# Gated attention: head 1's first half moved ahead of head 0's second half, with the norm of the second half of x between its products

## The chip, the cores and the metric

The kernel runs on one core of a Trainium2 chip. The metric is the time of one execution in device microseconds (us). Before the change the median of three runs is 2456.72 us (2456.72 to 2458.53).

## What is computed

The reference is a trunk of two layers on x (1024 tokens by 1024 features, float32). Layer 0 uses gated linear attention, layer 1 differential softmax attention; each is followed by a squared-ReLU MLP, and every sub-layer is normed and modulated by a conditioning vector. The change lies in layer 0's attention, with four heads, 128 key columns (DK) and 256 value columns (DV) each:

```python
h = rmsnorm(x, norm_g[i, 0]) * (1.0 + scale_t) + shift_t
q, k, v, r, a_lr = jnp.split(h @ w_in, [hk, 2 * hk, 2 * hk + D_MODEL, 2 * hk + 2 * D_MODEL], axis=-1)
log_a = jax.nn.log_sigmoid((a_lr @ w_a2 + b_a).astype(f32)) / GLA_TAU
...
b = jnp.cumsum(chunks(log_a, dk), axis=2)
scores = jnp.where(causal, jnp.einsum('bnchk,bnshk->bnhcs', q_dec, k_intra), 0.0)
o_intra = jnp.einsum('bnhcs,bnshv->bnchv', scores, v)
...
    o_c = jnp.einsum('bchk,bhkv->bchv', q_c, state)
    state = state * jnp.exp(decay)[..., None] + jnp.einsum('bchk,bchv->bhkv', k_c, v_c)
...
o = rmsnorm(o, norm_g).reshape(B, T, D_MODEL) * jax.nn.silu((r + b_r).astype(f32))
```

`a_lr` (16 columns, "rank") is shared by all heads; the state runs along the tokens, so a head's second half needs the state that its first half leaves.

## The kernel before, in words

**Units.** The 1024 tokens are two halves of 512 (four tiles of 128). A unit is one head on one half: 32 value parts (`v_part`, four tiles by eight row blocks of h), eight q parts and eight k parts (`qk_part`). Every product is three matmuls (`mm3`, L117 to L120) of the two-part split of its operands. The operands are split by `split` (L113 to L115): ScalarE writes the high part (L114), VectorE the low part (L115). A unit ends with the take-overs `take_v`, `take_q`, `take_k`, the decays (`decays`, L434: a product z, log-sigmoid, a scan and four exponentials), the turn of k (`turn_k`), the scores (`score`), four steps of output and state (`out_step`, L490, matmuls po and pu) with a norm of the output at the end (L525), and two turns of the output (`out_turn`, L529) that store it in `os_`.

**Order before.** Until about 64 us the prologue computes scale and shift and norms the first half of x. Then `first_unit` (L567) does head 0's first half, with all sums open at once: four value sums, q and k. It turns the rank columns, makes the decays, and calls `second_half` (L595), which norms the second half of x: squares by ScalarE, a broadcast of the reciprocal root, and for each of eight row blocks four transposes (L604), a copy to `xc` (L606), a store of `xc` to `xs` (L607) and three operations that write `h_hi` and `h_lo` (L611 to L613). Only then do `take_q`, `take_k`, `turn_k` and `score` of the first unit follow in the program. After that `stream` (L632) yields the units (0,1), (1,0), (1,1), (2,0) to (3,1) as (head, half), and two products of the gate r.

**What sets the order.** In the stream TensorE's order is written out by hand (`manual_schedule`, L647). The `Agenda` (L51) is a planner with a clock of its own: each part adds its cost to `now`, and steps such as `turn_k` or `out_step` are put in with a lag (`GLA_LAG`, L44) and emitted when they are due. The orders of the other engines, and TensorE's outside that block, are chosen by the compiler. Each engine works in the order so fixed.

**Buffers.** Split weights have five buffers (`wsp`, L89), raw ones two (`wraw`, L90). A unit pair needs four: two value tiles, q and k; the value tiles of head 0 carry the 16 rank columns as well (`gla_v`, L242). In PSUM `mm` has two buffers, `po` two, `pu` and `sc` one each, `tr` two. The four value sums of the first unit lie in `po`, `po`, `pu`, `sc`, its q and k in `mm`. The tiles of value, of the state S, and so on have the buffer counts of the pools `gu` and `gl`; `gl` and `ga` are opened when the pool `xb`, which holds the second half of x, is closed.

**ada blocks.** Beside the stream the rest of layer 0's modulation is computed in eight blocks (`ada_next`, L622): eight loads of 256 KB on POOL's queue, eight VectorE operations into one accumulator (L216 to L218, one buffer), then transposes and a sum (`ada_sums`, L222). The next block is begun when the last one's sums are emitted, 30.5 planner units after it began.

Of the kernel before, what the change touches and what calls it, by code (L numbers as in the profile page):

```python
# [21 lines left out]
P = 128  # L22
# [60 lines left out]
def trunk(ctx: ExitStack, tc, a, out):  # L83
# [157 lines left out]

    def gla_v(hd, i, pinned=False):  # L242
        w = a["gla_w_in"][0].rearrange("(k p) n -> p k n", p=P)[:, 4 * i:4 * i + 4, :]
        c0 = 1024 + hd * DV
        more = [w[:, :, 3072:3088]] if hd == 0 else []
        return [weight([w[:, :, c0:c0 + DV]] + more, [P, 4, DV + 16 * len(more)], pinned)]
# [16 lines left out]
    with tc.tile_pool(name="xa", bufs=4, reuse_waits="tile") as xa, \  # L263
# [57 lines left out]
        for blk in range(4):  # L321
# [16 lines left out]
            if blk == 0:  # L338
                bc = mm.tile([P, HT], F32, name="bc", tag="mm")
                broadcast(bc, rstd, 4)  # L340
                for k in range(KT):
                    tr = gp2.tile([P, HT], F32, name="tr", tag="tr", bufs=2)
                    for j in range(4):
                        pe.transpose(out=tr[:, j * P:(j + 1) * P], in_=xt[j][:, k * P:(k + 1) * P], identity=ident)
                    act.copy(out=xT[k], in_=tr)
                    dve.tensor_tensor(out=xn[k], in0=xT[k], in1=bc, op=ALU.mult)
                w_v0 += gla_v(0, 0, True)
            elif blk == 1:
                w_q0 = wcols(win, 0, DK, True)
            elif blk == 2:  # L350
                w_k0 = wcols(win, 512, DK, True)
                w_v0 += gla_v(0, 1, True)
            st = gp2.tile([P, 4], F32, name="st", tag="tr", bufs=2)
# [30 lines left out]
    with gla as g:  # L384
# [24 lines left out]
        def v_part(pv, half, w_v, j, k):  # L409
            agenda.now += 0.33  # L410
            hh, hl = h[k][half]
            wh, wl = w_v[k // 4]
            mm3(pv, hh[:, tiles[j]], hl[:, tiles[j]], wh[:, k % 4, :], wl[:, k % 4, :], k == 0, k == KT - 1)

# [4 lines left out]
        def take_v(u, pv, j):  # L419
            if u["hd"] == 0:  # L420
                if j == 0:
# [57 lines left out]
        def score(u):  # L479
# [5 lines left out]
            dve.copy_predicated(out=scz[u["half"]], mask=mk.bitcast(U32).broadcast_to([P, 4, P]), data=sc)  # L485
            agenda.add(lag["out"], out_step, u, 0)

        states = {}

        def out_step(u, j):  # L490
# [9 lines left out]
            if not (half == 1 and j == 3):  # L500
# [23 lines left out]
            for j in range(4):  # L524
                dve.tensor_scalar(out=ot[:, j, :], in0=ot[:, j, :], scalar1=rs[:, j:j + 1], scalar2=None, op0=ALU.mult)  # L525
            agenda.add(lag["turn"], out_turn, u, 0)
            agenda.add(lag["turn"] + 1.0, out_turn, u, 1)

# [9 lines left out]

        def unit(hd, half, ws):

            u = dict(hd=hd, half=half, v=[])
            w_v, w_q, w_k = ws
            if hd:
                agenda.add(lag["decay"], decays, u)
            for j in range(4):
                pv = mm.tile([P, DV + 16 if hd == 0 else DV], F32, name="pv", tag="mm")
# [4 lines left out]
            if hd == 0:  # L551
                agenda.add(lag["rank"], turn_at, u)
# [13 lines left out]

        def first_unit(between):  # L567
            u = dict(hd=0, half=0, v=[])
            pvs = [gp.tile([P, HT], F32, name="pv", tag=tag, bufs=bufs)[:, :DV + 16]
                   for tag, bufs in (("po", 2), ("po", 2), ("pu", 1), ("sc", 1))]  # L570
            pq, pk = (mm.tile([P, HT], F32, name=name, tag="mm") for name in ("pq", "pk"))
            for k in range(KT):
# [4 lines left out]
            for j in range(4):  # L577
                take_v(u, pvs[j], j)
            turn_at(u)
            decays(u)  # L580
            between()
            take_q(u, pq)
            take_k(u, pk)
            turn_k(u)
            score(u)

        with tc.tile_pool(name="xb", bufs=2, reuse_waits="tile") as xb:
            xt = []
# [4 lines left out]
            for k in range(KT):  # L593
                in_order(nc.sync.dma_start(out=xs[k, :, 0:HT], in_=xT[k]))
            def second_half():  # L595
                ssq = gt.tile([P, 4], F32, name="xssq", tag="ssq")
                rstd = gt.tile([P, 4], F32, name="xrstd", tag="rs")
                token_rms(xt, gt, ssq, rstd, xb.tile([P, D], BF16, name="junk", tag="xc"))
                bc = gp.tile([P, HT], F32, name="bc", tag="po", bufs=2)
                broadcast(bc, rstd, 4)  # L600
                for k in range(KT):
                    tr = gp2.tile([P, HT], F32, name="tr", tag="tr", bufs=2)
                    for j in range(4):
                        pe.transpose(out=tr[:, tiles[j]], in_=xt[j][:, k * P:(k + 1) * P], identity=ident)  # L604
                    xc = xb.tile([P, HT], F32, name="xc", tag="xc")
                    act.copy(out=xc, in_=tr)  # L606
                    nc.sync.dma_start(out=xs[k, :, HT:T], in_=xc)  # L607
                    hi, lo = hp.tile([P, HT], F32R, name="h_hi", tag="hhi"), hp.tile([P, HT], F32R, name="h_lo", tag="hlo")
                    h[k].append((hi, lo))
                    t = gt.tile([P, HT], F32, name="xh", tag="oT")  # L610
                    dve.scalar_tensor_tensor(out=t, in0=xc, scalar=gs[:, 0, k:k + 1], in1=bc, op0=ALU.mult, op1=ALU.mult)  # L611
                    act.activation(out=hi, in_=t, func=AF.Identity, bias=mod[:, 0, k:k + 1])
                    dve.scalar_tensor_tensor(out=lo, in0=t, scalar=mod[:, 0, k:k + 1], in1=hi.bitcast(F32),  # L613
                                             op0=ALU.add, op1=ALU.subtract)

            first_unit(second_half)

# [14 lines left out]
        def stream():  # L632

            for hd in range(GLA_H):
                ws = (gla_v(hd, 0) + gla_v(hd, 1), wcols(win, hd * DK, DK), wcols(win, 512 + hd * DK, DK)) if hd else \
                    (w_v0, w_q0, w_k0)
# [743 lines left out]
```

## Time and profile before

| | |
|---|---|
| median of three runs | 2456.72 us |
| the profiled execution, its own time | 2459.76 us |
| its span, first to last instruction | 2458.0 us |
| TensorE busy | 2381.5 us (97%) |
| VectorE busy | 1672.2 us (68%) |
| ScalarE busy | 999.1 us (41%) |
| mean granted TensorE clock | 0.988 |

Engines are written PE (TensorE), DVE (VectorE), ACT (ScalarE), POOL (GpSimd), SP (which issues DMAs). A wait is shown as the idle time of an engine before an instruction, with what released it. A clock of 1.00 is 2.4 GHz, 0.50 is 1.2 GHz.

### The profile page before, as it was taken

Reading aid. Unit: us, or ns where it says so; the run is one execution under the profiler, and the core shown is the slowest. Engines: PE = TensorE matmul, PEld = TensorE weight load, DVE = VectorE, ACT = ScalarE, POOL = GpSimd, SP = SyncE. Lnnn points to the kernel's source line nnn. Section 1 sums busy time; section 2 is a strip of 40 time slices with the busy share of each in tenths; the row PEclk is TensorE's granted clock in tenths of the full one; section 3 lists DMA queues with packets and bytes.
Section 4 is the critical chain, followed back from the end, with each engine's and each line's share of the span. In section 5 each row is a group of like instructions: output and inputs, shape, how many; then the busy total and the mean of one; then the engine's idle time right before and its main releaser. Section 6 shows DMA issues by size and latency. Waiting matters only on the chain.

```text
span 2458.0 us, 33452 instructions
## 1 busy us (share of the span) xinstructions
PE 2381.5 (97%) x12215; PEld 2051.2 (83%) x12215; DVE 1672.2 (68%) x3175; ACT 999.1 (41%) x1985; POOL 271.3 (11%) x482
## 2 busy tenths in 40 slices
PE   6899999999999999999999999999999999999998
PEld 5688878887888788888999999987788888888887
DVE  7777777666655666776787878788676656555444
ACT  5655556453332321212555555565553333222111
POOL 3011100001111201211221111120001111000000
PEclk8999999999999999999999999999999999999999
DMA  8333353524333844653211111024523334633111
GB/s 294 117 120 104 102 172 111 160 95 122 114 103 104 309 137 140 213 167 118 76 41 36 35 35 35 25 83 133 167 85 119 115 106 155 214 112 112 65 43 69
DMA packets 261925, 286.58 MB, mean 117 GB/s; under 512 B 15546, under 2 KB 200032, under 8 KB 261760
## 3 DMA queue, kind: packets, MB, share of 16 engines
q1 hardware_dynamic: 237120, 206.67, 26.8%
q0 software_dynamic: 23232, 75.53, 8.9%
q8 instruction: 96, 1.57, 0.3%
q10 hardware_dynamic: 1408, 2.24, 0.2%
q14 instruction: 69, 0.57, 0.1%
HBM read 222.52 MB, written 61.87 MB: 116 GB/s over the span
## 4 chain that ended last, share of the span: by engine, by line
PE 61%; issue 21%; DMA 7%; DVE 5%; ACT 3%; POOL 2%; POOLq 0%; DVEq 0%; SPq 0%; ACTq 0%
PE acc L118 10%; PE acc L119 10%; PE acc L120 10%; DMA ada_raw<-in_ada_w 4%; PE acc L859 3%; PE acc L860 3%; PE acc L861 3%; PE pp L118 3%; PE pp L120 3%; PE pp L119 3%; POOL hs L763 1%; DMA inner<-hs 1%; PE pr L118 1%; PE pr L120 1%; PE pr L119 1%
## 5 line engine op out<-in xcount | busy, mean ns | idle before, releaser
L114 ACT CAST whi<-raw 128x1024 fp32r<-128x1024 f32 (+3 forms) x217 | 209.1, 965 | 501.7 <-PE acc L119 276.8
L718 DVE SCALAR_TENSOR_TENSOR x<-acc,mod,x 128x512 f32<-128x512 f32 (+1 forms) x312 | 222.5, 720 | 221.2 <-PE acc L120 217.7
L118 PE MATMUL acc<-h_hi,whi 128*128 128x512 f32 x896 | 352.1, 393 | 2.4 <-DVE x L718 2.3
L119 PE MATMUL acc<-h_lo,whi 128*128 128x512 f32 x896 | 350.0, 391 | 0.0
L120 PE MATMUL acc<-h_hi,wlo 128*128 128x512 f32 x896 | 349.9, 390 | 0.0
L115 DVE TENSOR_TENSOR wlo<-raw,whi 128x1024 fp32r<-128x1024 f32 (+3 forms) x217 | 243.1, 1121 | 75.1 <-ACT whi L114 71.6
L118 PE MATMUL acc<-hd,whi 128*128 128x512 f32 (+1 forms) x576 | 212.2, 368 | 2.8 <-DVE x L718 2.8
L120 PE MATMUL acc<-hd,wlo 128*128 128x512 f32 (+1 forms) x576 | 211.2, 367 | 0.0
L119 PE MATMUL acc<-hd,whi 128*128 128x512 f32 (+1 forms) x576 | 211.2, 367 | 0.0
L118 PEld LDWEIGHTS acc<-h_hi,whi 128*128 128x128 f32 x896 | 168.7, 188 | 37.1 <-DVE x L718 3.4
L120 PEld LDWEIGHTS acc<-h_hi,wlo 128*128 128x128 f32 x896 | 168.6, 188 | 35.2
L119 PEld LDWEIGHTS acc<-h_lo,whi 128*128 128x128 f32 x896 | 168.7, 188 | 33.4
L118 PE MATMUL pp<-whi,h_hi 128*128 128x384 f32 x512 | 182.8, 357 | 0.7 <-ACT v L114 0.7
L859 PE MATMUL acc<-h_hi,whi 128*128 128x512 f32 x448 | 174.8, 390 | 0.0
L860 PE MATMUL acc<-h_lo,whi 128*128 128x512 f32 x448 | 174.7, 390 | 0.0
L861 PE MATMUL acc<-h_hi,wlo 128*128 128x512 f32 x448 | 174.0, 389 | 0.0
L120 PE MATMUL pp<-whi,h_lo 128*128 128x384 f32 x512 | 172.7, 337 | 0.0
L119 PE MATMUL pp<-wlo,h_hi 128*128 128x384 f32 x512 | 172.1, 336 | 0.0
L213 POOL DMA_DIRECT2D ada_raw<-in_ada_w x160 | 86.2, 539 | 534.0 <-DVE mod L230 318.9
L218 DVE SCALAR_TENSOR_TENSOR ada_acc<-ada_raw,cact,ada_acc 128x512 f32<-128x512 f32 x140 | 104.9, 749 | 52.4 <-DMA ada_raw<-in_ada_w 51.5
L861 PE MATMUL acc<-tq,wlo 128*128 128x512 f32 x336 | 132.0, 393 | 2.1 <-DVE wlo L115 2.1
L859 PE MATMUL acc<-tq,whi 128*128 128x512 f32 x336 | 131.7, 392 | 2.2 <-ACT part L870 2.2
(1802 smaller groups left out, 5257.9 us busy)
## 6 DMA issues: line engine op xcount, KB each, us to landing
raw<-in_mlp_w SPq DMA_DIRECT2D x128, 512.0 KB, 4.2
ada_raw<-in_ada_w POOLq DMA_DIRECT2D x160, 256.0 KB, 3.4
inner<-hs SPq DMA_DIRECT2D x128, 256.0 KB, 3.6
hs<-inner POOLq DMA_DIRECT2D x112, 256.0 KB, 3.0
x<-xs SPq DMA_DIRECT2D x64, 256.0 KB, 6.3
raw<-in_gla_w_in SPq DMA_DIRECT2D x24, 512.0 KB, 3.8
xs<-x SPq DMA_DIRECT2D x48, 256.0 KB, 3.0
raw<-in_diff_w_in SPq DMA_DIRECT2D x64, 192.0 KB, 2.9
```

The lines of the kernel that those rows point to most:

```text
L114: act.copy(out=hi, in_=src)
L115: dve.tensor_tensor(out=lo, in0=src, in1=hi.bitcast(F32), op=ALU.subtract)
L118: pe.matmul(out=o, lhsT=lh, rhs=rh, start=start, stop=False)
L119: pe.matmul(out=o, lhsT=lh, rhs=rl, start=False, stop=False)
L120: return pe.matmul(out=o, lhsT=ll, rhs=rh, start=False, stop=stop)
L213: queue.dma_start(out=w, in_=a["ada_w"][l].rearrange("(k p) n -> p k n", p=P)[:, k:k + kk, c0:c0 + n])
L218: dve.scalar_tensor_tensor(out=acc, in0=w[:, j, :], scalar=cact[:, k + j:k + j + 1], in1=acc, op0=ALU.mult, op1=ALU.add)
L718: return dve.scalar_tensor_tensor(out=t, in0=psum, scalar=mcols(l, gate)[:, kt:kt + 1], in1=t, op0=ALU.mult, op1=ALU.add)
L763: pool.dma_start(out=hs[f, :, half * HT:(half + 1) * HT], in_=r)
L859: pe.matmul(out=pt, lhsT=lh, rhs=rh, start=begin and k == 0, stop=False, skip_group_check=True)
L860: pe.matmul(out=pt, lhsT=lh, rhs=rl, start=False, stop=False, skip_group_check=True)
L861: pe.matmul(out=pt, lhsT=ll, rhs=rh, start=False, stop=k == K2 - 1, skip_group_check=True)
```

## The change

Head 1's first half is computed right behind head 0's first half, before the second half of x is there; the norm of the second half is cut into agenda steps that are emitted between the products of that unit. Then the stream does (1,1), (0,1), and (2,0) to (3,1).

```diff
-GLA_LAG = dict(rank=1.09, decay=4.71, keys=3.36, score=4.04, out=7.24, step=2.16, turn=14.56, ada=30.5)
+GLA_LAG = dict(first_keys=6.5, first_score=8.5, second_decay=12.0, x_norm=3.0, x_step=1.5, held=0.5, early_turn=7.0, second_out=15.0, rank=1.09, decay=4.71, keys=3.36, score=4.04, out=7.24, step=2.16, turn=14.56, ada=30.5)
...
+    ss = dram.tile([P, DV], F32, name="ss")
...
+            if u["hd"] == 0 and u["half"] == 1:
+                S = [gl.tile([P, DV], dt, name="S", tag=f"S{i}") for i, dt in enumerate((F32, F32R, F32R))]
+                nc.sync.dma_start(out=S[0], in_=ss)
+                split(S[1], S[2], S[0])
+                states[0] = S
+            if gl is None:
+                held.append(u)
+            else:
+                agenda.add(u["out"], out_step, u, 0)
...
-                split(Sn[1], Sn[2], Sn[0])
-                states[hd] = Sn
+                if hd == 0 and half == 0 and j == 3:
+                    nc.sync.dma_start(out=ss, in_=Sn[0])
+                else:
+                    split(Sn[1], Sn[2], Sn[0])
+                    states[hd] = Sn
...
-        def first_unit(between):
+        def first_unit():
...
+            pvs = [mm.tile([P, DV + 16], F32, name="pv", tag="mm") for _ in range(2)]
+            pvs += [gp.tile([P, HT], F32, name="pv", tag="po", bufs=2)[:, :DV + 16] for _ in range(2)]
+            pq, pk = (gp.tile([P, HT], F32, name=name, tag=tag) for name, tag in (("pq", "pu"), ("pk", "sc")))
...
-            turn_at(u)
+            agenda.add(lag["rank"], turn_at, u)
+            agenda.add(2 * lag["rank"], behind_first, u, pq, pk)
+
+        def behind_first(u, pq, pk):
             decays(u)
-            between()
             take_q(u, pq)
             take_k(u, pk)
-            turn_k(u)
-            score(u)
+            agenda.add(lag["first_keys"], turn_k, u)
+            agenda.add(lag["first_score"], score, u)
...
+                agenda.add(lag["x_norm"], spread, rstd)
+
+            def spread(rstd):
+                agenda.now += 0.9
                 bc = gp.tile([P, HT], F32, name="bc", tag="po", bufs=2)
                 broadcast(bc, rstd, 4)
                 for k in range(KT):
+                    agenda.add(k * lag["x_step"], turn_x, k, bc)
...
+            first_unit()
+            second_half()
+            w1 = (whole_v(1, True, True),)
+            for k in range(KT):
+                in_order(nc.sync.dma_start(out=xs[k, :, 0:HT], in_=xT[k]))
+            w1 += rest(1)
+            with tc.manual_schedule(engines={pe.engine}):
+                for n, _ in enumerate(unit(1, 0, w1, decay=lag["second_decay"])):
+                    while agenda.due() or n == 39 and not held:
+                        agenda.run()
+                while len(h[KT - 1]) < 2:
+                    agenda.run()
...
+            yield from unit(1, 1, w1, True)
+            yield from unit(0, 1, (whole_v(0), *rest(0)))
+            for hd in range(2, GLA_H):
+                ws = (whole_v(hd), *rest(hd))
                 for half in range(2):
-                    if hd or half:
-                        yield from unit(hd, half, ws)
+                    yield from unit(hd, half, ws)
...
             ada_next()
+            for u in held:
+                agenda.add(lag["held"], out_step, u, 0)
```

`turn_x` is the body of the old loop for one row block, unchanged. `whole_v` and `rest` are the loads of a head's two value tiles and of its q and k. The rank columns now come with head 1's value tiles, as a second load; unit (1,0) multiplies the first 256 columns alone, unit (1,1) all 272, unit (0,1) no longer has them. Head 0's state after the first half goes to DRAM (`ss`) and comes back before its second half; head 0's four weight tiles are loaded and split a second time for unit (0,1). The output turns of units (0,0) and (1,0) get a lag of 7.0 instead of 14.56. The stores of the first half of x to `xs` stand behind head 1's value loads on SP's queue.

## Rows read from the trace of the kernel before

**Rows 1.** The page's first part: busy time, share of the span, instructions.

```profile
PE 2381.5 (97%) x12215; PEld 2051.2 (83%) x12215; DVE 1672.2 (68%) x3175; ACT 999.1 (41%) x1985; POOL 271.3 (11%) x482
```

**Rows 2.** Windows: stretch, length, busy by engine, granted clock, DMA share, GB/s.

```profile
64.30:101.30 37.00, 26.52 (x165) 22.04 (x164) 29.70 (x51) 22.79 (x48) 5.87 (x11) 0.91 0.44 138
102.00:135.00 33.00, 31.08 (x194) 26.56 (x194) 27.07 (x49) 21.24 (x46) 2.26 (x5) 0.98 0.38 113
320.00:346.00 26.00, 21.86 (x109) 18.23 (x108) 16.61 (x37) 13.56 (x32) 2.77 (x5) 0.87 0.65 214
```

**Rows 3.** Windows: the two stretches at the lower clock.

```profile
75.80:82.50 6.70, 5.09 (x24) 4.60 (x23) 6.70 (x12) 6.54 (x13) 1.68 (x3) 0.50 0.44 155
339.40:345.40 6.00, 5.79 (x18) 4.78 (x19) 4.94 (x10) 2.00 (x3) 1.15 (x2) 0.50 0.81 281
```

**Rows 4.** Waits of TensorE between 60 and 345 us, the two longest.

```profile
PE tro L534 <- DVE ot L525: 4.1, 1, 4.1
PE tr L604 <- ACT xc L606: 4.1, 4, 2.8
```

**Rows 5.** Timeline of TensorE: start, busy, instruction, in the attention stage.

```profile
66.29 1.12 PE L439 MATMUL z<-aT,wa 16*128 16x512 f32 x2 [1.42 <-ACT aT L432]
...
69.59 1.09 PE L604 MATMUL tr<-ident,xt 128*128 128x128 f32 x8 [0.68 <-ACT xc L606]
...
111.81 0.39 PE L118 MATMUL pk<-h_hi,whi 128*128 128x512 f32 x1
...
117.25 0.28 PE L118 MATMUL pv<-whi,h_hi 128*128 128x256 f32 x1
...
120.00 0.28 PE L120 MATMUL pv<-whi,h_lo 128*128 128x256 f32 x1
```

**Rows 6.** VectorE's groups by shape, 62 to 102 us: busy, mean ns, idle before.

```profile
L611 DVE SCALAR_TENSOR_TENSOR xh<-xc,gs,bc 128x512 f32<-128x512 f32 x8 | 5.7, 742 | 0.1
L613 DVE SCALAR_TENSOR_TENSOR h_lo<-xh,mod,h_hi 128x512 fp32r<-128x512 f32 x8 | 5.7, 741 | 0.0
...
L115 DVE TENSOR_TENSOR vt<-pv,vt 128x256 fp32r<-128x256 f32 x7 | 2.8, 421 | 2.7 <-ACT vt L114 2.7
L115 DVE TENSOR_TENSOR wlo<-raw,whi 128x1024 fp32r<-128x1024 f32 x2 | 2.4, 1220 | 0.2 <-ACT whi L114 0.2
L462 DVE SCALAR_TENSOR_TENSOR ls<-pq,ls 128x512 f32<-128x512 f32 x2 | 1.3, 680 | 0.0
L441 DVE TENSOR_TENSOR_SCAN ls<-reset,ls 128x512 f32<-128x512 f32 x1 | 1.2, 1218 | 0.0
L380 DVE TENSOR_SCALAR ls<-z,colsT 128x512 f32<-128x512 f32 x1 | 0.7, 745 | 0.0
```

**Rows 7.** Window 62 to 92 us: VectorE's share where it is fullest (third busy number).

```profile
62.00:92.00 30.00, 21.49 (x128) 17.39 (x127) 25.67 (x44) 21.95 (x47) 3.29 (x6) 0.89 0.38 123
```

**Rows 8.** Timeline of VectorE: norms of two units' output, first and last operation.

```profile
112.38 0.14 DVE L153 TENSOR_SCALAR rs_m<-ssq 128x4 f32<-128x4 f32 x1
...
118.58 1.13 DVE L525 TENSOR_SCALAR ot<-ot,rs 128x256 f32<-128x256 f32 x4
...
149.01 0.17 DVE L153 TENSOR_SCALAR rs_m<-ssq 128x4 f32<-128x4 f32 x1 [0.34 <-ACT junk L518]
...
150.49 1.14 DVE L525 TENSOR_SCALAR ot<-ot,rs 128x256 f32<-128x256 f32 x4
```

**Rows 9.** Timeline of POOL: the first load of the seventh and of the eighth ada block.

```profile
303.84 0.54 POOL L213 DMA_DIRECT2D ada_raw<-in_ada_w  x1 [24.34 <-DVE mod L230]
...
331.70 0.54 POOL L213 DMA_DIRECT2D ada_raw<-in_ada_w  x1 [17.34 <-DVE mod L230]
```

**Rows 10.** Timeline of VectorE: last operation of the seventh block, two of the eighth.

```profile
312.79 0.74 DVE L218 SCALAR_TENSOR_TENSOR ada_acc<-ada_raw,cact,ada_acc 128x512 f32<-128x512 f32 x1
...
338.45 0.75 DVE L218 SCALAR_TENSOR_TENSOR ada_acc<-ada_raw,cact,ada_acc 128x512 f32<-128x512 f32 x1 [4.04 <-DMA ada_raw<-in_ada_w]
...
345.67 0.75 DVE L218 SCALAR_TENSOR_TENSOR ada_acc<-ada_raw,cact,ada_acc 128x512 f32<-128x512 f32 x1 [0.46 <-DMA ada_raw<-in_ada_w]
```

More of the change, by code (lines that the diff above doesn't have):

```diff
@@ L240, in mcols, with gla_v @@
         return mod[:, l, i * KT:(i + 1) * KT]
-    def gla_v(hd, i, pinned=False):
+    def gla_v(hd, i, pinned=False, rank=False):
         w = a["gla_w_in"][0].rearrange("(k p) n -> p k n", p=P)[:, 4 * i:4 * i + 4, :]
         c0 = 1024 + hd * DV
-        more = [w[:, :, 3072:3088]] if hd == 0 else []
+        more = [w[:, :, 3072:3088]] if rank else []
         return [weight([w[:, :, c0:c0 + DV]] + more, [P, 4, DV + 16 * len(more)], pinned)]
@@ L412, in v_part @@
             wh, wl = w_v[k // 4]
-            mm3(pv, hh[:, tiles[j]], hl[:, tiles[j]], wh[:, k % 4, :], wl[:, k % 4, :], k == 0, k == KT - 1)
+            n = slice(0, pv.shape[-1])
+            mm3(pv, hh[:, tiles[j]], hl[:, tiles[j]], wh[:, k % 4, n], wl[:, k % 4, n], k == 0, k == KT - 1)
         def qk_part(pt, half, w, k):
@@ L419, in take_v @@
         def take_v(u, pv, j):
-            if u["hd"] == 0:
+            if u["rank"]:
                 if j == 0:
@@ L537, in out_turn, with unit @@
             nc.sync.dma_start(out=os_[2 * hd + vh, :, half * HT:(half + 1) * HT], in_=oT)
-        def unit(hd, half, ws):
-            u = dict(hd=hd, half=half, v=[])
+        def unit(hd, half, ws, rank=False, decay=None):
+            first = (hd, half) == (1, 0)
+            u = dict(hd=hd, half=half, v=[], rank=rank, out=lag["second_out" if first else "out"],
+                     turn=lag["early_turn" if first else "turn"])
             w_v, w_q, w_k = ws
-            if hd:
-                agenda.add(lag["decay"], decays, u)
+            if not rank:
+                agenda.add(decay or lag["decay"], decays, u)
             for j in range(4):
-                pv = mm.tile([P, DV + 16 if hd == 0 else DV], F32, name="pv", tag="mm")
+                pv = mm.tile([P, DV + 16 if rank else DV], F32, name="pv", tag="mm")
                 for k in range(KT):
@@ L550, in unit @@
                 take_v(u, pv, j)
-            if hd == 0:
+            if rank:
                 agenda.add(lag["rank"], turn_at, u)
@@ L565, in unit @@
             agenda.add(lag["score"], score, u)
-        def first_unit(between):
[L568 to L571, printed above, removed]
+        def first_unit():
+            u = dict(hd=0, half=0, v=[], rank=True, turn=lag["early_turn"])
+            pvs = [mm.tile([P, DV + 16], F32, name="pv", tag="mm") for _ in range(2)]
+            pvs += [gp.tile([P, HT], F32, name="pv", tag="po", bufs=2)[:, :DV + 16] for _ in range(2)]
+            pq, pk = (gp.tile([P, HT], F32, name=name, tag=tag) for name, tag in (("pq", "pu"), ("pk", "sc")))
             for k in range(KT):
@@ L601, in second_half @@
                 for k in range(KT):
[L602 to L614, printed above, removed]
@@ L616, in trunk, with turn_x @@
-            first_unit(second_half)
+                    agenda.add(k * lag["x_step"], turn_x, k, bc)
+            def turn_x(k, bc):
+                agenda.now += 0.45
+                tr = gp2.tile([P, HT], F32, name="tr", tag="tr", bufs=2)
+                for j in range(4):
+                    pe.transpose(out=tr[:, tiles[j]], in_=xt[j][:, k * P:(k + 1) * P], identity=ident)
+                xc = xb.tile([P, HT], F32, name="xc", tag="xc")
+                act.copy(out=xc, in_=tr)
+                nc.sync.dma_start(out=xs[k, :, HT:T], in_=xc)
+                hi, lo = hp.tile([P, HT], F32R, name="h_hi", tag="hhi"), hp.tile([P, HT], F32R, name="h_lo", tag="hlo")
+                h[k].append((hi, lo))
+                t = gt.tile([P, HT], F32, name="xh", tag="oT")
+                dve.scalar_tensor_tensor(out=t, in0=xc, scalar=gs[:, 0, k:k + 1], in1=bc, op0=ALU.mult, op1=ALU.mult)
+                act.activation(out=hi, in_=t, func=AF.Identity, bias=mod[:, 0, k:k + 1])
+                dve.scalar_tensor_tensor(out=lo, in0=t, scalar=mod[:, 0, k:k + 1], in1=hi.bitcast(F32),
+                                         op0=ALU.add, op1=ALU.subtract)
```

20 lines of the change are left out of this document (9 added, 11 removed).

## The prediction, made before the changed kernel ran

> **What bounds the kernel now.** I read the page's busy times first: TensorE is busy 97% of the span [rows 1], so a change that leaves its products as they are can only win back its idle time and what it runs at the lower clock. Then the windows, to see where those lie. From the end of the first unit's products at 64.3 us to 101.3 us TensorE is busy 26.52 of 37.00 us: 10.5 us idle [rows 2]. In 75.8 to 82.5 us the granted clock is 0.50, its level of 1.2 GHz, after a stretch in which TensorE was mostly idle; the 5.09 us busy there would take half at 2.4 GHz, so 2.5 us more are lost [rows 3]. The change can win at most these 13.0 us at that place. The second loss of the stage is its tail: 4.1 us idle between 320 and 346 us and 2.9 us (half of 5.79) at the lower clock behind it [rows 2, 3].
>
> The list of waits says why. In the first place TensorE waits for ScalarE's copies `xc` of the second half's norm [rows 4]: nothing else can run there, because head 0's second half needs that norm. VectorE is busy 25.67 of 30.00 us in 62 to 92 us [rows 7], so the norm and the first unit's take-overs are its work more than TensorE's. At the tail the wait is for the normed output, `ot` [rows 4], and VectorE itself stood 4.04 us in its order before an ada operation whose load had not landed [rows 10].
>
> **The change, part by part.** *The unit (1,0) fills the gap.* It needs only the first half of x, which is there. Its 24 matmuls of one tile of values take 2.87 us (117.25 to 120.12), four tiles 11.5; its 24 matmuls of k take 5.44 us (111.81 to 117.25), q and k 10.9 [rows 5]. With it TensorE must do the two decays' z (2.2, two of 1.1), eight blocks of four transposes (1.09 us for eight, so 4.4) [rows 5], and, by estimate from the same rows, the rank turn, the broadcast, the turn of k and the twelve score matmuls, 3.7 together. That is 32.7 us: without a stall TensorE is through at 64.3 + 32.7 = 97.0 us.
>
> *VectorE's share of it.* Before unit (1,1) may write its first sum it has to do: the second half's norm 11.4 (5.7 + 5.7), eight low parts of v 3.2 (2.8/7 each), two decays 8.0 (a scan 1.2 and four operations at 0.7 each), the first unit's `take_q` 2.7, `take_k` 2.1, turned k 0.7 and masked scores 0.7, four low parts of head 1's weights 4.8 (2.4/2 each), the two q products of unit (1,0) 1.3, small ones 0.8. The sum is 35.7 us [rows 6]. Begun at 62.5 us it ends at 98.2 us, 1.2 us behind TensorE. The two engines come out almost level, and the order is fixed on each, so a stall on one is soon a stall on the other. The lower bound of TensorE's idle time is 1.2 us; for the upper one VectorE works at its 86% of [rows 7]: 35.7/0.86 = 41.5, end at 104.0, 7.0 us idle. I take 4.0, the middle, because TensorE now has products of its own beside every wait for `xc`, while the turn of k and the scores still stand in its order behind a VectorE chain. Gain: 13.0 - 4.0 = 9.0 us, if the clock stays at 2.4 GHz.
>
> The Trainium skill, page "Perfetto Trace Analysis", section "Identifying Performance Opportunities", says that where the most contended engine changes over time, interleaving the regimes may improve performance. By it the stretch would cost the longer of the two sums, 98.2 us, and the gain would be 11.8. In this trace, where VectorE is busy 27.07 of 33.00 us beside a full TensorE (102 to 135 us), TensorE still lost 1.9 us [rows 2]; I go by that and by the bounds above.
>
> *Weights twice.* Head 0's four tiles come again for unit (0,1): four loads of 512 KB and four casts on ScalarE and VectorE; 4.8 us on VectorE by [rows 6]. The cover is VectorE's idle time beside units (1,1) and (0,1): 5.9 of 33 us in a like stretch [rows 2], and part of it is owed to the backlog of (1,0). Bounds 0 and 4.8; I take 1.5, nearer to nothing. The loads themselves have 0.38 DMA share beside them there [rows 2]. *Head 1's weights early.* Two value loads, with two more for the rank columns, now stand on SP's queue before the eight stores of the first half to `xs`. What is queued behind them are those stores, and behind these q and k. Of the stores only the buffers of `h_lo` for the second half wait, not needed before about 70 us. At the 281 GB/s of a loaded stretch [rows 3] their 1.1 MB are 3.9 us; I cost it at nothing, between 0 and 3.9, since the first unit's products hide it.
>
> *State of head 0.* One store of 128 KB, one load in its place before (0,1)'s output, one split for one split: nothing, with a whole unit's products in between. The load stands in SP's queue ahead of weights for head 2, for which a unit's time is left. *Early turns.* A unit's output norm takes 119.71 - 112.38 = 7.3 us beside a full VectorE and 2.6 us otherwise (first operation to the last's end) [rows 8]; the planner now asks for it 7.0 units behind the last step instead of 14.56. Two turns, each between 0 and 1.5; I take 0.5 in all. *Decays of (1,0)* reuse the one buffer of two temporaries, free when the first unit's keys are turned; that is already in the stall.
>
> *The tail.* By the planner's own clock ada's first block begins at the stream's start, its seventh 6 x 30.95 later at the soonest. The stream is one unit shorter; adding up all costs and lags, the seventh block, begun inside the stream before (planner 213.0, end of stream 232.7), is begun behind its end (238.8, against 236.8). So two blocks, not one, are left for the tail, one after the other, as they share an accumulator. Taken alone that is no cost: the products of the gate r stand free to fill. I leave the tail's 7.0 us as they are; bounds in the rivals.
>
> **Sum** against the profiled execution's own 2459.76 us: -9.0 + 1.5 + 0.5 = -7.0, so 2452.8 us. The profiled execution is 3.0 us above the median of the runs shown, 2456.72; on that scale the forecast is 2449.7 us. A measurement of this kernel can tell about 0.2% from no change, 4.9 us.
>
> **Rivals.** *VectorE becomes the bound* (no change). The 35.7 us run at 86%, and the backlog costs the full 4.8 of the doubled weights and 1.5 at the turns: 13.0 - 7.0 - 4.8 - 1.5 = -0.3, 2456.4 us. For it: VectorE's own sum is as long as TensorE's, and in 102 to 135 us it is already 82% busy. Against: ada's first block, which stood in this stretch, now comes behind it. This is also the case in which the change does not do what it says: TensorE would wait for the same `xc` copies and key turns, only inside unit (1,0). Chance 0.25.
>
> *The tail turns on ada* (slower). The seventh block took 313.53 - 303.84 = 9.7 us, the eighth, beside the loads of the gate stage, 346.42 - 331.70 = 14.7 [rows 9, 10]. If the compiler's order puts the eighth block's transposes before products that could run, TensorE stands the 14.7 us that the second of two successive blocks lasts, and runs some 2.9 at the lower clock again: -7.0 + 14.7 + 2.9 = +10.6, 2467 us. It decides from 11.9 us of new wait on. For it: the wait for `ot` in [rows 4] is of this kind. Against: before, the eighth block's transposes came behind the tail with TensorE full from 340 us on. Chance 0.15. The Trainium skill, "TensorE: Matmul & The Clock Gate", section "Part 2: What happens when you issue a matmul", says that matmuls stay in program order; the trace agrees, with 4.1 us spent before `tro`.
>
> *All hides and the tail's stall goes too* (faster still). The seventh block now starts before the loads of the gate stage, so `ot` need not wait for it: 11.8 + 7.0 = -18.8, 2438 us. For it: the stall hung on one late load. Chance 0.12.
>
> **How the numbers follow.** The forecast's own case, 2449.7 with 2446 to 2454, has 0.48; about seven tenths of it lie beyond 4.9 us. Faster: 0.34 + 0.12 and a little of the first rival, 0.49. Same: 0.14 + 0.21, 0.35. Slower: 0.16. The range reaches to 2441 on the low side, short of the last rival's full price, and to 2462 on the high side, past the first rival and into the second; about 0.2 is left out. The likeliest case alone is 2446 to 2454.
>
> **What would show it.** Right: from 64 us TensorE goes on with `pv` of (1,0); its idle time up to the end of that unit's k is near 4 us; the clock stays at 1.00 there; VectorE is nearly full to 98 us or later; unit (1,1) begins near 101. Wrong: idle time of 7 us or more there, with waits of `trk` or `sc` for VectorE; new waits of `tro` for `ot` in unit (1,1); a first `pv` of (1,0) later than 65 us because a value weight was not cast; TensorE idle in the tail before `ada_st` or `tro` for more than the 4.1 us of before.

## The result, and the profile after

The changed kernel takes 2473.35 us (median of four runs, 2469.5 to 2476.38) beside 2457.62 us for the kernel before on the same chip (four runs, 2456.72 to 2460.3): a ratio of 1.0061, interval 1.0048 to 1.0074. That is 15.7 us slower, where 7 us faster was forecast, and outside the range. The profiled execution takes 2470.89 us, its span 2469.2 us, at a mean granted clock of 0.99.

The page's busy line, which answers to [rows 1]:

```profile
PE 2380.7 (96%) x12215; PEld 2053.8 (83%) x12215; DVE 1674.6 (68%) x3179; ACT 1003.6 (41%) x1989; POOL 270.2 (11%) x482
```

TensorE does the same 12215 instructions in 0.8 us less; what has grown is its idle time. VectorE and ScalarE have four instructions more each, the second split of head 0's weights (2.4 and 4.5 us more busy time). Windows that answer to [rows 2] (stretch, length, busy by engine in the order PE, PEld, DVE, ACT, POOL, granted clock, DMA share, GB/s):

```profile
64.50:102.00 37.50, 27.35 (x169) 24.52 (x169) 31.48 (x50) 27.93 (x53) 1.68 (x3) 0.82 0.45 143
111.00:145.30 34.30, 34.30 (x234) 30.95 (x233) 23.51 (x46) 20.92 (x55) 1.08 (x2) 1.00 0.28 89
319.50:372.00 52.50, 44.38 (x220) 36.58 (x218) 33.51 (x64) 22.87 (x45) 6.99 (x13) 0.93 0.55 180
```

The first stretch is as empty as it was (10.15 us idle in 37.5; before 10.5 in 37.0), although unit (1,0) now stands in it. Unit (1,1) behind it runs without a gap (second line). In the tail (third line) 8.1 us are idle. TensorE's waits from 20 to 400 us (total, times, longest), which answer to [rows 4]:

```profile
PE pv L119 <- DVE vt L116: 14.3, 3, 6.6
PE tro L547 <- DVE ot L538: 8.9, 2, 5.6
...
PE ada_st L227 <- DVE ada_acc L219: 3.5, 1, 3.5
...
PE tr L635 <- ACT xc L637: 2.5, 1, 2.5
```

Where they stand, in TensorE's timeline (the wait is in the brackets):

```profile
64.33 0.28 PE L119 MATMUL pv<-whi,h_hi 128*128 128x256 f32 x1
...
82.06 0.58 PE L119 MATMUL pv<-whi,h_hi 128*128 128x256 f32 x1 [6.62 <-DVE vt L116]
...
159.59 1.03 PE L547 MATMUL tro<-ident,ot 128*128 128x128 f32 x4 [3.35 <-DVE ot L538]
...
197.99 0.42 PE L119 MATMUL pv<-whi,h_hi 128*128 128x256 f32 x1 [2.57 <-DVE vt L116]
...
235.56 0.43 PE L119 MATMUL pv<-whi,h_hi 128*128 128x256 f32 x1 [5.10 <-DVE vt L116]
...
354.23 0.66 PE L547 MATMUL tro<-ident,ot 128*128 128x128 f32 x2 [5.57 <-DVE ot L538]
...
372.98 1.09 PE L227 MATMUL ada_st<-ident,ada_acc 128*128 128x128 f32 x4 [3.53 <-DVE ada_acc L219]
```

Unit (1,0) does begin right behind the first unit. Most of the new waits are far from the edited stretch, among units whose code is the same. To place them I cut each run at three marks of TensorE's timeline: the end of the first unit's last k product (64.4 us before, 64.5 after), of the fourth unit in the order (184.0, 182.5), of the last unit, (3,1) (309.7, 319.5), and the first product of the output projection (413.1, 428.7). Each stretch holds the same units in both orders:

| us | three units of heads 0, 1 | (2,0) to (3,1) | tail |
|---|---|---|---|
| before | 119.6 | 125.7 | 103.4 |
| after | 118.0 | 137.0 | 109.2 |
| difference | -1.6 | +11.3 | +5.8 |

The sum is 15.5 us. The two profiled executions differ by 11.1 us, because outside the marks the changed one was 4.4 us shorter. That rest lies anywhere between 2103 and 2116 us in the profiles of this document, in kernels that hardly differ there. Stretches are therefore compared by the marks, which come from one profile of each kernel, and whole kernels by their medians.

What VectorE does before the wait of 5.10 us:

```profile
226.80 0.75 DVE L381 TENSOR_SCALAR ls<-z,colsT 128x512 f32<-128x512 f32 x1
227.46 0.74 DVE L219 SCALAR_TENSOR_TENSOR ada_acc<-ada_raw,cact,ada_acc 128x512 f32<-128x512 f32 x1
228.13 0.69 DVE L382 TENSOR_TENSOR ls<-ls,ls 128x512 f32<-128x512 f32 x1
228.94 0.75 DVE L219 SCALAR_TENSOR_TENSOR ada_acc<-ada_raw,cact,ada_acc 128x512 f32<-128x512 f32 x1
229.61 1.22 DVE L443 TENSOR_TENSOR_SCAN ls<-reset,ls 128x512 f32<-128x512 f32 x1
...
232.26 0.75 DVE L219 SCALAR_TENSOR_TENSOR ada_acc<-ada_raw,cact,ada_acc 128x512 f32<-128x512 f32 x1 [0.18 <-DMA ada_raw<-in_ada_w]
232.93 0.68 DVE L452 TENSOR_TENSOR t<-ls 128x512 f32<-128x512 f32 x1
234.42 0.75 DVE L219 SCALAR_TENSOR_TENSOR ada_acc<-ada_raw,cact,ada_acc 128x512 f32<-128x512 f32 x1 [0.81 <-DMA ada_raw<-in_ada_w]
235.09 0.42 DVE L116 TENSOR_TENSOR vt<-pv,vt 128x256 fp32r<-128x256 f32 x1
```

An ada block's products and the unit's decays stand alternately in VectorE's order, some products wait for their own load as well, and the low part of a finished value tile (`vt`) stands behind all of it. TensorE's next value tile needs that tile's PSUM buffer. In the tail it is the block's loads: on VectorE the last two products of the seventh block wait 4.01 and 2.45 us for theirs, ahead of the `ot` that the turn at 354.23 us needs.

```profile
346.99 0.75 DVE L219 SCALAR_TENSOR_TENSOR ada_acc<-ada_raw,cact,ada_acc 128x512 f32<-128x512 f32 x1 [4.01 <-DMA ada_raw<-in_ada_w]
...
350.27 0.75 DVE L219 SCALAR_TENSOR_TENSOR ada_acc<-ada_raw,cact,ada_acc 128x512 f32<-128x512 f32 x1 [2.45 <-DMA ada_raw<-in_ada_w]
...
353.74 1.14 DVE L538 TENSOR_SCALAR ot<-ot,rs 128x256 f32<-128x256 f32 x4
```

So the theory to test: **the loss is the blocks' place.** The first block begins at the stream's start, which now comes 12.8 us later (its first product stands at 101.7 us on VectorE, before at 88.9), and each next one a fixed lag later, so all blocks fall elsewhere in the units. By the planner, blocks began at +3.4, +6.0 and +8.9 us to the z of units (1,1), (2,0), (2,1) before; after, at -4.7, -1.2 and +2.1 us to the z of (2,0), (2,1), (3,0), and two blocks instead of one begin in the tail. The rival: the new order costs by itself (weights twice, the state through DRAM, early turns).

### The profile page after: what moved, and what is told of

Same layout as the page of the kernel before. It is cut to its first block, busy times and chain, and to the rows that moved or that the text cites. A ratio compares the mean times of both kernels' runs of the same rounds, so it can differ in the third digit from the quotient of the medians.

```text
span 2469.2 us, 33482 instructions
## 1 busy us (share of the span) xinstructions
PE 2380.7 (96%) x12215; PEld 2053.8 (83%) x12215; DVE 1674.6 (68%) x3179; ACT 1003.6 (41%) x1989; POOL 270.2 (11%) x482
## 4 chain that ended last, share of the span: by engine, by line
PE 78%; issue 7%; DVE 7%; DMA 5%; ACT 3%; POOL 0%; DVEq 0%; SPq 0%; ACTq 0%; POOLq 0%
PE acc L119 12%; PE acc L120 12%; PE acc L121 12%; PE acc L903 7%; PE acc L905 7%; PE acc L904 7%; PE pp L119 3%; PE pp L121 3%; PE pp L120 3%; DMA ada_raw<-in_ada_w 2%; DVE wlo L116 1%; ACT et L1172 1%; PE at L1202 1%; PE bc L165 1%; PE pr L121 1%
## 5 line engine op out<-in xcount | busy, mean ns | idle before, releaser
L120 PEld LDWEIGHTS acc<-h_lo,whi 128*128 128x128 f32 x896 | 168.7, 188 | 33.5
```

Of the source, the lines that this page charges most:

```text
L120: pe.matmul(out=o, lhsT=lh, rhs=rl, start=False, stop=False)
```

## Experiments: one lag at a time

Four runs of the changed kernel with only numbers of `GLA_LAG` changed; the kernel before beside them 2459.42 us.

```diff
e1_ada26:  -ada=30.5           +ada=26.0
e2_xstep3: -x_step=1.5         +x_step=3.0
e3_turn:   -early_turn=7.0     +early_turn=14.56
e4_three:  all three
```

**e1_ada26.** 

> The changed kernel with the lag between ada blocks cut from 30.5 to 26.0 planner units, nothing else. By the planner's lags the blocks then begin 7 to 15 units behind a unit's decays instead of within 5 units of three of them, and one block instead of two is begun behind the stream. Theory A (the loss sits where an ada block meets a unit's decays and value take-over on VectorE, and in the tail): the waits of pv for vt at 195 and 230 us (2.6 and 5.1) and of ada_st (3.5) go, with the lower clock behind them some 14 us in all; 2457 to 2462 us. Theory B (VectorE has too much work throughout since the weights are cast twice): the waits move and stay as long; 2470 to 2476 us.

**e2_xstep3.** 

> The changed kernel with the steps of the second half's norm 3.0 instead of 1.5 planner units apart. Theory A (in the early unit it is the order, all eight row blocks ahead of the fourth value sum, that overfills VectorE for a while): the wait of 6.6 us for vt at 82 us shrinks below 3, the unit's k ends near 104 instead of 110.9 us; 2464 to 2469 us. Theory B (VectorE's own sum of work bounds the early unit): the unit still ends at 109 us or later; 2470 to 2476 us.

**e3_turn.** 

> The changed kernel with the output turns of units (0,0) and (1,0) at the old lag of 14.56 planner units instead of 7.0. If the wait of 3.4 us of tro for ot at 156 us is this lag's, it goes with about 1 us of lower clock behind it, and nothing takes its place: 2466 to 2471 us. If VectorE is only late as a whole, another wait of the same length stands near 160 us: 2470 to 2476 us.

**e4_three.** 

> All three at once: ada lag 26.0, x step 3.0, early turn 14.56. If the three losses are separate and all placement, the gains add up (14 + 6 + 4): 2447 to 2452 us, faster than the kernel before the change by some 6 to 10 us. If VectorE's total bounds the stage, 2460 us or more.

| us | time | ratio, interval | heads 0, 1 | (2,0) to (3,1) | tail |
|---|---|---|---|---|---|
| e1_ada26 | 2464.58 | 1.0022 [1.0013, 1.0032] | 117.8 | 135.0 | 104.9 |
| e2_xstep3 | 2472.74 | 1.0054 [1.0038, 1.0070] | 115.4 | 137.2 | 108.7 |
| e3_turn | 2474.76 | 1.0065 [1.0050, 1.0080] | 118.5 | 137.1 | 110.9 |
| e4_three | 2465.59 | 1.0026 [1.0014, 1.0037] | 119.1 | 133.2 | 107.4 |

Only the blocks' lag moves the time, by about 9 us, so neither the early turns nor the pace of the norm is the loss. e1 lies between the figures of its two theories. e4 was expected at 2447 to 2452 us: the gains did not add up, and its time alone would speak for the rival, VectorE's total; f2 below decides that. In e2 the wait on `vt` did not shrink (6.9 us), yet unit (1,0) took 42.8 us instead of 46.5, which h2 below takes up. In e1 both late waits on `vt` (197.99 and 235.56 us) go, but a block now falls on the taking up of (0,1)'s k, whose PSUM buffer unit (2,0) needs for its values; (2,0) then takes 40.4 us:

```profile
188.76 0.58 PE L119 MATMUL pv<-whi,h_hi 128*128 128x256 f32 x1 [3.68 <-DVE t L470]
```

In e3 the wait at 159.59 us goes and others of 0.6 to 1.3 us come, with no gain in time. VectorE did four of the block's products between the first operation of that output's norm (151.38 us) and its `ot` (159.09 us); in f2 below, without blocks, the same early turns wait only 0.2 us.

## Experiments: the blocks taken away, and the old order with the new places

The kernel before beside these four: 2459.78 us.

```diff
f1_before_noada, f2_after_noada:
-        ada_todo = [(0, c0) for c0 in range(2048, 6144, 512)]
+        ada_todo = []
f3_before_shift (the kernel before):
-            ada_next()
+            agenda.add(22.0, ada_next)
f4_after_tied (the changed kernel), in decays:
+            if pend:
+                agenda.add(4.0, ada_next, pend.pop())
```

f1 and f2 also drop the first call of `ada_next` and set the sums that it would have written to zero, so these two, and all later runs built on f2, leave out part of the computation; they serve as yardsticks only. In f4 `ada_next` leaves its block in `pend` instead of adding the fixed lag, except for the last two.

**f1_before_noada.** 

> The kernel before, with the eight ada blocks of the attention stage left out (their sums are set to zero, so the gates and the MLP's shift and scale of layer 0 are zero). It is the yardstick for the next run. Both theories expect it below the kernel before: eight sums of 0.45 us leave TensorE (3.6 us), and the tail no longer waits for the last block; 2440 to 2455 us.

**f2_after_noada.** 

> The changed kernel with the same eight ada blocks left out. Theory (the reordering is sound, and what it lost is where its ada blocks fall): without any block the new order is 2 to 9 us faster than the old order without any block, and units (2,0) to (3,1) take within 1 us what they take there. Rival (the new order itself costs: weights twice, the state's way through DRAM, early turns): it stays 8 to 16 us slower than the old order without blocks.

**f3_before_shift.** 

> The kernel before with one number added: the first ada block starts 22.0 planner us later, so that the planner's blocks stand at -4.4, -1.2, +2.1 and +5.2 us to the gate products of units (2,0) to (3,1) and at +2 and +33 us behind the stream's end, where the changed kernel has -4.7, -1.2, +2.1, +5.2, +2 and +33. Theory (the blocks' place is the loss): the old order now loses as the new one did, 10 to 17 us, 2468 to 2476 us, with the tail about 4 us longer and units (2,0) and (2,1) 3 to 7 us longer. Rival (the new order costs): no more than the second tail block's 4 us, 2456 to 2463 us.

**f4_after_tied.** 

> The changed kernel with each ada block tied to a unit's gate product (4.0 planner us behind it, where the kernel before had most of its own at +3.4 to +11.5) in place of the fixed lag of 30.5. Seven blocks then start in the stream and one behind it, as in the kernel before. Theory (the blocks' place is the loss): units (2,0) to (3,1) within 1.5 us of the kernel before's 31 us and the tail at 104 us, so 2452 to 2460 us. Rival (the new order costs): 2466 to 2474 us.

| us | time | ratio, interval | heads 0, 1 | (2,0) to (3,1) | tail |
|---|---|---|---|---|---|
| f1_before_noada | 2438.87 | 0.9911 [0.9898, 0.9923] | 111.0 | 121.2 | 95.3 |
| f2_after_noada | 2438.98 | 0.9915 [0.9902, 0.9928] | 111.3 | 121.2 | 95.3 |
| f3_before_shift | 2472.69 | 1.0053 [1.0041, 1.0065] | 116.6 | 135.9 | 110.6 |
| f4_after_tied | 2463.39 | 1.0018 [1.0009, 1.0028] | 120.4 | 129.3 | 103.5 |

This settles the sign. Without blocks the two orders take the same time; the old order with the new order's block places is as slow as the changed kernel, and with the same waits at the same work. TensorE's waits in f3:

```profile
PE pv L118 <- DVE vt L115: 9.7, 3, 5.5
...
PE tro L534 <- DVE ot L525: 5.2, 1, 5.2
...
PE ada_st L226 <- DVE ada_acc L218: 3.9, 1, 3.9
```

The rival falls, and so does half of the forecast: f2 is not 2 to 9 us ahead of f1. f4 (between the theory's and the rival's figures) brings the later units and the tail back near their old length, but unit (1,1), which got two blocks close on each other, took 40.3 us.

A block has a price far above TensorE's part in it, which is 32 transposes of 0.27 us in all, 8.7 us even without overlap. Eight blocks cost 20.9 us in the old order (2459.78 to 2438.87) and 34.4 us in the changed one (2473.35 to 2438.98, measured at different times; 36.5 by the marks). In the tail alone, none is 95.3 us; runs that begin one block there take 103.4 (before) to 107.4 us (e4), those that begin two 108.7 (e2) to 110.9 us (e3).

## Experiments: the early unit

Left was why the new order gives back the whole early gap even without blocks. In f2 unit (1,0) takes 45.8 us, 9.85 of them idle (first window), with the same wait of 6.62 us on `vt`; in f1 and f2 a later unit without blocks runs full (second window, f2):

```profile
65.50:111.30 45.80, 35.95 (x211) 31.35 (x210) 33.53 (x54) 30.35 (x56) 0.00 (x0) 0.89 0.31 101
267.70:298.00 30.30, 30.30 (x204) 27.42 (x204) 20.39 (x39) 17.66 (x41) 0.00 (x0) 1.00 0.24 70
```

Two causes were left: VectorE's work is the bound, or the two written orders put late things ahead of ready ones. g4 and g3 also move the tied blocks from 4.0 to 8.0. Beside g1 to g4 the kernel before took 2457.89 us, beside h1 to h3 2458.53.

```diff
g1_late_qk (f2 and this):
             decays(u)
-            take_q(u, pq)
-            take_k(u, pk)
+            agenda.add(2.5, take_q, u, pq)
+            agenda.add(4.0, take_k, u, pk)
g2_late_qk_weights (g1 and this):
-            w1 += rest(1)
+            agenda.add(6.0, lambda: w1.extend(rest(1)))
...
g4_tied8 (f4 and this):
-                agenda.add(4.0, ada_next, pend.pop())
+                agenda.add(8.0, ada_next, pend.pop())
g3_tied8_late: g4 with g2's edits
h2_lags_alone (f2 and this), h1_early_lags (g2 and this), h3_tied8_early (g3 and this):
-first_keys=6.5, first_score=8.5, second_decay=12.0, x_norm=3.0, x_step=1.5
+first_keys=10.0, first_score=12.0, second_decay=16.0, x_norm=3.0, x_step=2.5
```

**g1_late_qk.** 

> The changed kernel without ada blocks (as f2), and the first unit's q and k products are taken up 2.5 and 4.0 planner us behind its gate product instead of at once, so that unit (1,0)'s first vt is issued to VectorE ahead of them. Theory (the order on VectorE makes the 6.6 us wait of unit (1,0)'s third value tile): the wait falls to about 3 us, unit (1,0) ends some 3 us earlier, 2435 to 2438 us. Rival (VectorE, 98% busy there, is the bound, so that what is put ahead of one wait is behind the next): the wait moves, the unit's end and the time stay, 2438 to 2440 us.

**g2_late_qk_weights.** 

> As g1, and head 1's q and k weights are loaded and split 6.0 planner us behind the first unit instead of at once, which takes their low parts (1.2 us each) from ahead of the vt too. Theory: the wait falls below 1.5 us, unit (1,0) ends 5 us or more earlier than in f2, 2431 to 2437 us. Rival (VectorE is the bound): 2438 to 2440 us; or the weights come late for the q product at the unit's third fifth, a wait on wlo, 2438 to 2443 us.

**g3_tied8_late.** 

> The changed kernel with the edits of g2 and all eight ada blocks, each tied to a unit's gate product at 8.0 planner us behind it. Theory: what g4 gives less what g2 gained on f2, 2450 to 2458 us, so that the new order is level with the kernel before or ahead of it. Rival (VectorE is the bound in the early stretch): as g4.

**g4_tied8.** 

> The changed kernel as f4, with the blocks 8.0 instead of 4.0 planner us behind each gate product. In f4 unit (1,1) took 40.3 us with two blocks close on each other and a wait of 3.4 us on the state; 4 us later the second block should clear that. Theory (blocks' place): unit (1,1) back to 34 to 36 us, the later units 31 to 33 us each, 2455 to 2461 us. Rival (two blocks in one unit cost wherever they stand): (1,1) stays at 38 us or more, or (0,1) takes the loss over, 2462 to 2466 us.

**h1_early_lags.** 

> The changed kernel without ada blocks, with g2's two edits, and later due times in the early stretch: k turned 10.0 and scores 12.0 planner us behind the first unit's gate product (6.5 and 8.5), the second gate product at 16.0 (12.0), a piece of x every 2.5 (1.5). Theory A (TensorE stood in unit (1,0) because its order put turned pieces and k ahead of value tiles that were ready, while VectorE was late): the 6.6 us wait goes, idle time between 64 and 112 us falls from 10 or 11 us to under 5, unit (1,0) ends 40 to 43 us after the first unit's products instead of 46 to 48, and the time is 2430 to 2435 us. Theory B (VectorE's work is the bound of the stretch, in whatever order): it ends no earlier than 45 us after them, 2436 to 2440 us.

**h2_lags_alone.** 

> The changed kernel without ada blocks and with the four later due times of h1 alone; q, k and the weights are taken up at once, as in f2. Theory A: the wait on vt (6.6 us) stays, since the same VectorE work stands ahead of that vt, but what is behind it runs closer; the unit ends 43 to 45 us after the first unit's products, 2433 to 2437 us. Theory B: 45 us or more, 2436 to 2440 us.

**h3_tied8_early.** 

> The changed kernel with all ada blocks, tied at 8.0 us behind each gate product as in g3, and the early edits of h1. Theory A: what h1 gains on f2 comes on top of g4's 2457.6 us, 2450 to 2455 us, ahead of the kernel before. Theory B: as g3 and g4, 2457 to 2460 us.

| us | time | ratio, interval | unit (1,0) | heads 0, 1 | (2,0) to (3,1) | tail |
|---|---|---|---|---|---|---|
| g1_late_qk | 2439.73 | 0.9924 [0.9904, 0.9944] | 48.1 | 113.7 | 121.6 | 95.3 |
| g2_late_qk_weights | 2436.36 | 0.9908 [0.9893, 0.9923] | 46.5 | 112.1 | 121.8 | 95.3 |
| h2_lags_alone | 2434.55 | 0.9908 [0.9893, 0.9923] | 41.5 | 107.1 | 121.1 | 95.3 |
| h1_early_lags | 2432.01 | 0.9899 [0.9885, 0.9913] | 40.7 | 106.3 | 121.2 | 95.3 |
| g3_tied8_late | 2458.86 | 1.0007 [0.9998, 1.0017] | 46.6 | 118.5 | 124.7 | 105.8 |
| g4_tied8 | 2457.59 | 0.9999 [0.9990, 1.0009] | 47.9 | 121.5 | 124.5 | 104.8 |
| h3_tied8_early | 2452.88 | 0.9978 [0.9969, 0.9987] | 41.1 | 112.3 | 124.6 | 105.5 |

g1 and g2 went against my theory of that moment: the wait on `vt` fell and another came (g1, the first two lines; g2, the third), and the unit ended no earlier. The median of g2 lies in the theory's range, but not by way of the unit.

```profile
79.46 0.58 PE L120 MATMUL pv<-whi,h_hi 128*128 128x256 f32 x1 [2.83 <-DVE vt L117]
...
85.55 0.63 PE L478 MATMUL trk<-ident,t 128*128 128x128 f32 x4 [2.95 <-ACT h_hi L644]
```

```profile
83.69 1.09 PE L478 MATMUL trk<-ident,t 128*128 128x128 f32 x4 [6.58 <-DVE t L470]
```

That looked like a full VectorE. But the new wait is at `trk`, the turn of k, which the planner had put into TensorE's order ahead of a value tile that needed nothing. With later due times for the turn, the scores, the second z and the pieces of x the same VectorE work lies in a shorter unit (h1, then h2):

```profile
63.80:104.50 40.70, 34.18 (x210) 29.89 (x210) 33.53 (x53) 29.90 (x56) 0.00 (x0) 0.92 0.36 113
```

```profile
64.00:105.50 41.50, 33.34 (x210) 29.03 (x210) 33.66 (x53) 30.29 (x56) 0.00 (x0) 0.92 0.35 111
```

VectorE is busy 33.53 us in f2's 45.8 us and 33.53 us in h1's 40.7 us: the amount was not the bound of that unit, the order was (theory A). Not as expected: the wait on `vt` stays at 5.44 us in h1 (7.07 in h2), and 6.5 us are idle where under 5 were forecast. What went is the waiting behind it and part of the lower clock.

```profile
83.02 0.58 PE L120 MATMUL pv<-whi,h_hi 128*128 128x256 f32 x1 [5.44 <-DVE vt L117]
```

VectorE works without a gap ahead of that `vt`, from 70.8 us on; whether another order of its own would shorten this wait, no run shows. By the marks h1 is 4.7 us ahead of f1 in the first stretch and level behind it (121.2 and 95.3 us in both, as in f2). By the medians it is 6.9 us, but the two ratios' intervals overlap, so the size rests on the marks.

g4 did what it should for the later units (124.5 us) and for unit (1,1) (35.0 us), but (0,1) took the loss over, 38.6 us, as its rival said; its median is in the theory's range all the same. g3 came out as g4, as its rival said. h3 carries the early lags to the kernel with all its work and is ahead of both kernels.

## Experiments: how much of that is the blocks' place

```diff
i1_before_tied8: the kernel before, with g4's tie
k1_last_block (h3 and this):
-                    agenda.add(lag["ada"], ada_next, pend.pop())
+                    agenda.add(15.0 if ada_todo else lag["ada"], ada_next, pend.pop())
```

**i1_before_tied8.** 

> The kernel before, in its own order and with its own due times, but with each ada block tied to a unit's gate product, 8.0 planner us behind it, as in g4 and h3. With seven gate products in its stream all eight blocks start in the stream and none in the tail. Theory C (a block's place is a term of its own, whatever the order): the tail falls from 103.4 us towards the 95.3 us that it takes without blocks, units (2,0) to (3,1) stay at 123 to 126 us, and the time is 2447 to 2453 us, level with h3 or ahead of it. Theory D (h3 owes its 5.6 us to the new order, since the old order's blocks already stood well): 2455 to 2460 us.

**k1_last_block.** 

> h3 with one number changed: its eighth ada block starts 15.0 planner us behind the seventh instead of 30.5, so about 12 planner us ahead of the stream's end instead of 4 behind it. Theory C (a block that stands in the tail costs 8 to 10 us there, whatever the order): the tail falls from 105.5 us to between 96 and 100, 2444 to 2449 us, ahead of h3 and of the old order with tied blocks (i1, 2454.2). Rival (the block only takes its cost along, into unit (3,1)'s keys and output steps on VectorE): the tail falls, but unit (3,1) or the tail's first steps lose as much, 2451 to 2455 us.

| us | time | before beside it | ratio, interval | heads 0, 1 | (2,0) to (3,1) | tail |
|---|---|---|---|---|---|---|
| i1_before_tied8 | 2454.22 | 2458.25 | 0.9988 [0.9978, 0.9999] | 120.5 | 125.5 | 96.3 |
| k1_last_block | 2448.51 | 2456.77 | 0.9965 [0.9951, 0.9979] | 113.9 | 123.8 | 101.5 |

i1's time lies between what C and D expected, and its interval overlaps h3's: of h3's gain of 5.6 us the blocks' place alone gives 4.0 in the old order; its marks are C's: the tail falls to 96.3 us in the old order too. h3 is 8.2 us shorter than i1 among heads 0 and 1 and 9.2 us longer in the tail, where its eighth block stands. k1 moves that block ahead of the stream's end and is the fastest version with all its work, 8.3 us below the kernel before. Its tail, at 101.5, did not fall below 100 as expected. The interval of k1 just touches that of i1, so that the new order is worth something with all its work is likely, but not certain. The rival's share shows as one wait in the tail, where the last product of the eighth block stands ahead of the state `S`:

```profile
PE pu L119 <- DVE S L520: 2.2, 1, 2.2
```

## Why the prediction was wrong

**The step that failed first: the ada blocks were treated as cover that costs nothing.** The text counted where the seventh block falls ("two blocks, not one, are left for the tail ... Taken alone that is no cost"), and never asked where the others fall in their units. Both were in its reach: the planner sum that gave 238.8 for the seventh block gives -4.7 and -1.2 us to a unit's z for the third and fourth. The sign stood in the trace of before, where the one block begun close behind a z (+0.8, unit (1,0)) had one wait of the same kind:

```profile
PE pv L118 <- DVE vt L115: 1.8, 1, 1.8
```

By the marks this place cost +11.3 us in (2,0) to (3,1) and +5.8 us in the tail; f3 shows both without the change's order, f1 and f2 show neither without blocks.

**The second step: "I take 4.0" for the stall in unit (1,0).** The sums of work were right: for TensorE 32.7 us forecast, 33.34 us busy in h2, part of it at the lower clock; for VectorE 35.7 us up to (1,1)'s first sum, 33.5 in unit (1,0) without blocks. The idle time in the changed kernel's unit (1,0) was 10.15 us, above the upper bound of 7.0, because both ends of the range came from the amount of work; the order, which is fixed on both engines, was left out. The text had named the risk ("the turn of k and the scores still stand in its order behind a VectorE chain") without a price. So the gain of 9.0 was nothing at the end of (1,0): its 46.5 us are 9.8 more than the 36.7 forecast, 6.15 of them idle time and 3.65 busy time (36.35 us for 32.7), part of it at the lower clock, which the sum put at nothing ("if the clock stays at 2.4 GHz"). At the fourth unit's end 1.6 us were left, where 7 were forecast, though one ada sum less stands there. Of the signs of being wrong that were named, the idle time of 7 us or more came, with a wait for `vt` in place of `trk` or `sc`, and so did the longer waits in the tail.

The Trainium skill, "Perfetto Trace Analysis", section "Identifying Performance Opportunities", was weighed with 98.2 us as the end of the stretch. The best early stretch here ended at 104.5 us (h1, without blocks): interleaving paid, once the written order allowed it, but not to the longer of the two sums, which was the prediction's own reading.

**The small terms.** *Weights twice*: 1.5 taken; in f2 unit (0,1) takes 31.3 us where f1's units behind the first gap take 30.3 to 30.6, so at most 1.0. *Head 1's weights early*: nothing taken; one wait of 0.6 us on `wlo` near 67 us, found in every trace of the new order. *State*: nothing, and none seen. *Early turns*: 0.5 taken; without blocks 0.2 us of waits (`tro` in f2), with a block ahead of `ot` 3.35.

**The rivals.** "The tail turns on ada" named the right resource and one of the right places: `ada_st` waits 3.53 us, and `tro` 5.57 instead of 4.1. Its price of 14.7 us was too high for the tail (5.8), and it had no term for the units ahead. The price itself was read a little short: [rows 9] are the fourth loads of their blocks, not the first, since three loads are issued as the block before ends (310.83 to 313.83 us for the eighth); from its first product at 330.93 us the eighth block lasted 15.5 us. "VectorE becomes the bound" gave no change, which f2 shows without blocks, but for another reason than its own. "All hides" failed on its condition: the seventh block still met late loads in the tail, and the turn waited 5.57 us.

## What to carry to other kernels

Background work on a fixed period is tuned to the order that it runs beside: a change that moves its start, or the work's length, needs the new place of every piece worked out against the chains of the same engine, and a look at each coincidence in the old trace. Tie such pieces to an event of the foreground instead (here: 8 planner us behind a unit's gate product), and end them before the tail. Where two engines with fixed orders feed each other, sums of work give only the lower bound of a stretch; walk both orders for the first thing that stands behind a late one.

## What the runs showed of the hardware that was not expected

In the changed kernel each wait of over 2.4 us between 64 and 430 us brought a stretch at the lower clock with it. Behind the wait of 5.10 us TensorE ran 3.4 us at 1.2 GHz, and behind the one of 3.35 us 3.2 us, both windows full of work:

```profile
235.60:239.00 3.40, 3.40 (x17) 3.40 (x18) 1.09 (x2) 0.63 (x1) 0.94 (x2) 0.52 0.48 147
160.70:163.90 3.20, 3.20 (x18) 3.20 (x17) 3.20 (x6) 1.81 (x4) 0.00 (x0) 0.50 0.69 255
```

So a wait of 5.1 us cost about 6.7 (half of 3.4 more), one of 3.35 about 4.95, by estimate from these rows. The length of a wait does not settle it: behind f3's wait of 3.00 us at 197.50 us the clock stays at 1.00 (first line), behind the kernel before's 1.84 us at 132.60 us it falls to 0.50 (second line).

```profile
197.50:201.00 3.50, 3.50 (x29) 3.50 (x30) 1.96 (x4) 3.06 (x7) 0.00 (x0) 1.00 0.52 180
133.80:137.20 3.40, 3.40 (x19) 3.40 (x18) 2.28 (x5) 1.03 (x3) 1.57 (x3) 0.50 0.69 221
```

From f2 to h2 idle time in unit (1,0) falls by 1.7 us (9.85 to 8.16) and busy time for as many matmuls by 2.6 us (35.95 to 33.34), with the granted clock up from 0.89 to 0.92: more came back from the clock than from the idle time.
